# VectorE's 16 counting instructions moved from ahead of its first cast to behind its last

## The chip, the cores and the metric

The kernel runs on one core of one Trainium2 chip. The metric is the time of one execution in device microseconds; lower is better.

## The reference, cut to what matters

```python
batch, m, k, n = 16, 512, 768, 1024
# x: (batch, k, m) float32, y: (batch, k, n) float32
def reference(x, y):
    return np.einsum('bkm,bkn->bmn', x, y).astype(np.float32)
```

These are sixteen matrix products. Each loads 1.5 MB of x and 3 MB of y and stores 2 MB.

## The kernel before

SyncE issues all loads and stores. VectorE (DVE) casts each x and y tile to bfloat16. GpSimd (POOL) turns the casts' counter into one that TensorE (PE) can take from. TensorE multiplies in a loop, and ScalarE (ACT) copies the sums from PSUM to an output buffer. VectorE and ScalarE each count a semaphore `idle` up 16 times at their start. No instruction waits for it.

```python
def load(b):                                   # SyncE
    i = b % 2
    if b >= 2:
        nc.sync.wait_ge(cast, nx[b - 2])       # x buffer read by its cast
    wide_dma("x", xs[i][:], x_v[b], 4, True).then_inc(sx[i], 16)
    if b >= 2:
        nc.sync.wait_ge(cast, nx[b - 2] + parts(b - 2))
    wide_dma("y", ys[i][:], y_v[b], 2, True).then_inc(sy[i], 16)
# ... stores in batches of four, the last ones single ...

for _ in range(16):                            # VectorE
    nc.vector.sem_inc(idle, 1)
for b in range(B):
    i = b % 2
    n = 16 * (b // 2 + 1)
    if b >= 2:
        nc.vector.wait_ge(groups, 2 * (b - 1))
    nc.vector.wait_ge(sx[i], n)
    nc.vector.tensor_copy(xb[:, i], xs[i][:]).then_inc(cast, 1)
    nc.vector.wait_ge(sy[i], n)
    for h in range(parts(b)):                  # two parts for the last b, one before
        ks = slice(h * KT // parts(b), (h + 1) * KT // parts(b))
        nc.vector.tensor_copy(yb[:, i, ks], ys[i][:, ks]).then_inc(cast, 1)
# ... GpSimd and TensorE ...

nc.scalar.nop().then_inc(room, 2)              # ScalarE
for _ in range(16):
    nc.scalar.sem_inc(idle, 1)
# ... 32 copies PSUM -> ob ...
section.close()                                # a barrier of all engines
nc.sync.dma_start(o_v[B - 1, :, HB:], ob[(B - 1) % NO][:, HB:])   # the final store
```

## Time and profile before

| | before |
|---|---|
| time | 260.58 us, median of 3 (260.51 to 260.74) |
| span, first to last instruction of the profiled run | 258.8 us |
| bytes moved, mean rate | 109.07 MB, 421 GB/s |
| VectorE busy | 82.0 us, 32% |
| mean granted TensorE clock | 0.887 |

The page gives busy times by engine, then 40 slices of the span, then the transfer queues, then the chain of work that ended last. Here is the chain of the kernel before in order of time (start in us, duration in us, what).

```profile
225.47 0.27 issue
225.74 23.56 PE ps L162 x96
249.30 0.02 issue
249.32 1.86 ACT ob L178
```

The reader is to see that the last work is TensorE's matmuls of the last two batches, 48 each, and a ScalarE copy. The final store follows. VectorE's last cast lies outside of this chain.

Here is the view of SyncE's waits of before (who waited for whom: us in total, times, longest), the lines about the end:

```profile
SPq L47 <- ACTq L47: 1.9, 1, 1.9
...
SPq L47 <- PEq L47: 0.8, 1, 0.8
```

Line 47 is the barrier that closes the section, ahead of the final store. SyncE waited there for ScalarE and TensorE and not for VectorE.

### The profile page before, as it was taken

The page shows a single profiled execution, that of the slowest core. Times are in us where ns is not written, and L with a number is a line of the kernel's source. Part 1 is how long each engine was busy: PE and PEld are TensorE (multiplying, and loading weights), DVE is VectorE, ACT ScalarE, POOL GpSimd, SP SyncE. Part 2 cuts the span into 40 slices and gives each one's busy share as a digit, 9 for nine tenths or more (in the row PEclk, how much of TensorE's full clock was granted, in tenths as well). Part 3 has the DMA queues.
Part 4 walks back from the last instruction along what each step waited for, and adds up shares of the span by engine and source line. Part 5 has one row for each costly group of instructions (what it writes and reads, how often), then busy time and mean ns, then how long its engine had stood idle before and what let it go on. Part 6 is the DMA issues. An engine that isn't in the chain of part 4 may idle for free. (4 is left out here: it accounts for less than half of the span.)

```text
span 258.8 us, 2419 instructions
## 1 busy us (share of the span) xinstructions
PE 178.6 (69%) x768; PEld 88.8 (34%) x768; DVE 82.0 (32%) x33; ACT 60.9 (24%) x33; POOL 0.2 (0%) x4
## 2 busy tenths in 40 slices
PE   0019999999999007996599800999579970199950
PEld 0004555555544003553255400455235530045520
DVE  0271644527255250021643624002345272300000
ACT  1000432243220004234022002224302200413430
POOL 0000000000000000000000000000000000000000
PEclk9999999999999756999799975699979995569995
DMA  6999989898999999999999999999899999999996
GB/s 262 444 479 395 486 365 486 365 486 380 471 403 448 377 420 438 453 458 418 433 433 418 441 387 436 420 463 471 380 486 387 463 395 399 436 433 420 441 415 265
DMA packets 4658, 109.07 MB, mean 421 GB/s; under 512 B 784, under 2 KB 784, under 8 KB 784
## 3 DMA queue, kind: packets, MB, share of 16 engines
q1 hardware_dynamic: 4656, 109.06, 98.6%
q14 instruction: 2, 0.02, 0.0%
HBM read 75.50 MB, written 33.55 MB: 421 GB/s over the span
## 5 line engine op out<-in xcount | busy, mean ns | idle before, releaser
L162 PE MATMUL ps<-yb,xb 128*128 x768 | 178.6, 397 | 70.7 <-PEq L157 70.6
L162 PEld LDWEIGHTS ps<-yb,xb 128*128 x768 | 88.8, 116 | 160.0 <-issue 88.5
L178 ACT COPY ob<-ps 128x2048 f32<-128x2048 f32 x32 | 59.6, 1872 | 188.3 <-PE ps L162 126.4
L140 DVE CAST yb<-ys 128x6144 bf16<-128x6144 f32 (+1 forms) x17 | 53.8, 3171 | 80.1 <-DMA ys<-in_y_dram 80.1
L136 DVE CAST xb<-xs 128x3072 bf16<-128x3072 f32 x16 | 28.2, 1760 | 60.0 <-DMA xs<-in_x_dram 48.8
L178 ACT ACT_TABLE_LOAD x1 | 1.3, 1283 | 2.0 <-issue 2.0
L209 POOL MEMSET const-bfloat16-1.0<- 128x1 bf16 x1 | 0.1, 101 | 0.0
L209 POOL MEMSET const-uint8-127<- 128x1 uint8 x1 | 0.1, 101 | 0.0
L209 POOL MEMSET const-float32-0.0<- 128x1 f32 x1 | 0.1, 98 | 0.2 <-issue 0.2
L209 POOL MEMSET const-float32-1.0<- 128x1 f32 x1 | 0.1, 98 | 0.0
## 6 DMA issues: line engine op xcount, KB each, us to landing
ys<-in_y_dram SPq DMA_DIRECT2D x16, 3072.0 KB, 18.6
out_dram<-ob SPq DMA_DIRECT2D x15, 2048.0 KB, 27.4
xs<-in_x_dram SPq DMA_DIRECT2D x16, 1536.0 KB, 20.1
out_dram<-ob SPq DMA_DIRECT2D x2, 1024.0 KB, 7.9
```

Of the source, the lines that this page charges most:

```text
L136: nc.vector.tensor_copy(xb[:, i], xs[i][:]).then_inc(cast, 1)
L140: nc.vector.tensor_copy(yb[:, i, ks], ys[i][:, ks]).then_inc(cast, 1)
L162: mm = nc.tensor.matmul(ps[g][:, m, nt], x_w[:, bass.ds(s, 1), kt, mo], yb[:, bass.ds(s, 1), kt, nt * NF:(nt + 1) * NF], start=(kt == 0), ...
L178: cp = nc.scalar.copy(ob[b % NO][:, g * HB:(g + 1) * HB].rearrange("p m (t f) -> p m t f", f=NF), ps[g][:])
L209: nc = _bacc.Bacc("TRN2", target_bir_lowering=False, num_devices=1)
```

## The change

The intent is to let VectorE go to its first cast without counting first, and to count when its casts are done.

```diff
-    for _ in range(16):
-        nc.vector.sem_inc(idle, 1)
     for b in range(B):
         i = b % 2
         n = 16 * (b // 2 + 1)
@@
         for h in range(parts(b)):
             ks = slice(h * KT // parts(b), (h + 1) * KT // parts(b))
             nc.vector.tensor_copy(yb[:, i, ks], ys[i][:, ks]).then_inc(cast, 1)
+
+    for _ in range(16):
+        nc.vector.sem_inc(idle, 1)
```

## The prediction

> **What bounds the kernel now.** I read the page of the profile first, from its DMA rows: if the transfers fill the span, only something that moves them can matter.

> ```profile
> span 258.8 us, 2419 instructions
> PE 178.6 (69%) x768; PEld 88.8 (34%) x768; DVE 82.0 (32%) x33; ACT 60.9 (24%) x33; POOL 0.2 (0%) x4
> ...
> DMA  6999989898999999999999999999899999999996
> ...
> q1 hardware_dynamic: 4656, 109.06, 98.6%
> q14 instruction: 2, 0.02, 0.0%
> ```

> The reader is to see that the packets of the one data queue account for 98.6% of the span on 16 transfer engines, that only the first and the last of the 40 slices are clearly below full, and that VectorE (DVE) is busy for a third of the time. The kernel must move 75.50 MB in and 33.55 MB out, 109.05 MB; over the 258.8 us that is 421 GB/s. A core that is full of transfers from about 2 us to the last packet gets no shorter because an engine that waits for transfers is freed from some of its own instructions.

> Next I read the windows by stage, to see whether any stage is held by something else. Columns are PE, weight load, DVE, ACT and POOL busy with instruction counts, the granted clock, the DMA share and GB/s.

> ```profile
> 0.00:7.10 7.10, 0.00 (x0) 0.00 (x0) 0.00 (x0) 1.28 (x1) 0.20 (x4) 1.00 0.72 280
> 7.10:18.30 11.20, 0.00 (x0) 0.00 (x0) 5.34 (x3) 0.00 (x0) 0.00 (x0) 1.00 1.05 454
> ...
> 225.70:251.40 25.70, 23.54 (x96) 11.34 (x96) 0.00 (x0) 8.91 (x5) 0.00 (x0) 0.89 1.00 429
> 251.40:258.80 7.40, 0.00 (x0) 0.00 (x0) 0.00 (x0) 0.00 (x0) 0.00 (x0) 0.51 0.67 281
> ```

> The reader is to see that the DMA share is about 1.00 in the stage before the matmuls and also in the last stage with matmuls; that DVE does nothing in the first 7.1 us, which is where the 16 instructions stand now; and that it does nothing after 225.7 us, which is where they will stand. The chain that ended last names PE for its last 23.56 us, then a ScalarE copy, then the final store; no VectorE instruction is on it.

> Then the two places themselves, in three views: the lines of the counting instructions, the timeline of VectorE and SyncE at the start, and the timeline of VectorE near the end.

> ```profile
> L129 DVEq EVENT_SEMAPHORE  x16: 21/21/21, 1.0 to 2.4; - x16
> ```
> ```profile
> 0.95 0.39 SPq L75 DMA_DIRECT2D xs<-in_x_dram  x1
> ...
> 7.11 1.76 DVE L136 CAST xb<-xs 128x3072 bf16<-128x3072 f32 x1 [7.11 <-DMA xs<-in_x_dram]
> ```
> ```profile
> 218.65 3.43 DVE L140 CAST yb<-ys 128x3072 bf16<-128x3072 f32 x2 [4.92 <-DMA ys<-in_y_dram]
> ```
> ```profile
> L47 DVEq DRAIN  x1: 17/17/17, 248.5 to 248.5; - x1
> ```

> The 16 instructions start from 1.0 to 2.4 us. The first cast starts at 7.11 us and was waiting for its load, which SyncE issued at 0.95 us. The last two casts end at 218.65 + 3.43 = 222.08 us, and the next thing VectorE's queue does is a drain at 248.5 us, part of the barrier at the end of the section.

> [...] 21 ns are reported for each, but the starts are (2.4 - 1.0) / 15 = about 93 ns apart, so I cost them at the spacing and not at the reported duration. [...] I take the measured 421 over the span as what full looks like here. [...] The trace shows that queue with two packets, 0.02 MB in all, against 109.06 MB of data. No trace here says which engine asked for them.

> **The change, part by part.** It removes nothing and adds nothing; the number of instructions stays at 2419.

> Taken from the front: 16 x 93 ns = 1.5 us of VectorE's sequencer, between 1.0 and 2.4 us. After it, that sequencer stood until 7.11 us at the wait of the first cast, so 7.11 - 2.4 - 0.09 = 4.6 us of slack lay behind the counting. The cast is released by the landing of the first x tile, and SyncE, not VectorE, issues that load, at 0.95 us. VectorE will reach its wait 1.5 us earlier and stand there 1.5 us longer. Gain on the path: 0.

> Added at the back: the same 1.5 us behind the last cast. The semaphore waits that VectorE's queue does by itself (line 135) start about 0.3 us behind the end of the cast before them (29.1 against 25.39 + 3.36 = 28.75), so I put the 16 at about 222.4 to 223.9 us. The drain of the barrier comes at 248.5 us: 24.6 us of slack, 16 times what they need. The casts have incremented their own semaphore by then, so the last matmuls are not held. Cost on the path: 0.

> Who waits for the counter: nobody. The only uses of the semaphore in the program are these 16 increments and 16 on ScalarE; no wait names it. Its value can release nothing earlier or later.

> Between the two places: the casts keep their order, waits and semaphores. Load issues that wait for casts (the longest waits of SyncE: 110.9 us for the y casts, 68.4 us for the x casts) therefore come at the same times, unless the first cast moves, which it does not. Sum: 0.0 us, hence the time before, 260.58, written as 260.6.

> **The rivals.**

> *The first casts start earlier.* If the start were bound by VectorE's sequencer, up to 1.5 us, 0.6% of 260.58, could be had. Against it: the view of waits gives the load as what ended the 7.11 us of idle time, and even the 0.95 us issue is SyncE's. A gain at the start would also have to survive the full transfers of the rest. A little of it could still be real: the first four load issues take 0.39 to 0.70 us, later ones 0.47, and 16 fewer increments fly about in those microseconds. I give that at most 0.2 us, because the first issue, the quickest of them, sets when data starts. It would make about 260.4.

> *The tail becomes longer.* If VectorE came late to the closing barrier, the last store would be issued later by that. For that the counting would have to take over 24 us in place of 1.5. SyncE's waits at the barrier (view of SyncE's waits) are for ScalarE, 1.9 us, and PE, 0.8 us, and none for VectorE. If all 1.5 us stood on the path nevertheless, the time would be 262.1, still within 2%.

> *The fetch of instructions moves.* The stream behind the 16 instructions lies 16 places further ahead, so if one of the two packets is VectorE's, it will come at another time. The two hold 0.02 MB / 2 = about 8 KB each; a transfer engine moves 421 / 16 = 26 GB/s, so one packet is about 0.3 us of one of 16 engines. A transfer waits for the slowest of its 16, so up to 0.3 us either way: 260.3 to 260.9. This is the rival I hold most likely to be visible at all. If a fetch were to stop VectorE before a cast for some microseconds, it would be hidden or not by the 3.5 to 5.6 us for which VectorE waits for each y load in any case; behind the last cast it would meet the 24.6 us of slack.

> *The clock.* TensorE's granted clock is 0.887 of full on average. Nothing here changes the matmuls, so I expect the same, and the transfers hide part of it anyway.

> **How the range and the chances follow.** The three runs before lie between 260.51 and 260.74, 0.23 us apart. Around 260.6 I allow for that spread, 0.3 us for the fetch, 0.2 us at the start, and some drift between chips: 260.0 to 261.2. Two per cent are 5.2 us, more than three times all that the moved instructions take together. For "faster" or "slower" something would have to happen that no view shows; I give 0.01 and 0.02, the slower one more because an unforeseen stop of the queue can only cost. The rest, 0.97, is "same".

> **What would show each step right or wrong.** Right at the start: the first x cast again begins near 7.1 us, with the load as releaser, and the first matmul near 18.3 us. Right at the end: the 16 instructions sit between about 222.4 and 223.9 us, about 93 ns apart, the drain of VectorE again near 248.5 us, and SyncE's waits at the barrier name ScalarE and PE only. Right in between: the data queue near 98.6% and 421 GB/s. Wrong: a first cast ahead of 6.5 us, a VectorE queue that reaches the barrier last, or casts in the middle that wait for something other than loads and PE. What would make the number wrong by per cents is a different order of loads and stores in the transfer queue, set off by a small shift; the last stage with ScalarE waiting up to 21.7 us for a store is the place that I would look at first.

"That queue" is q14 of the page, with its two packets. The 421 GB/s that it takes as full are the mean of the span and its own estimate of what full is; the windows of before give 425 to 434 GB/s in the three long stages and 454 from 7.1 to 18.3 us. That a transfer waits for the slowest of its 16 is seen at the final store of before: its 16 landings came from 256.25 to 258.04 us, and SyncE's wait for it was passed at 258.06 us. The 0.2 us at the start and the drift between chips were guesses; in the rounds of e1 to e12 the medians of the kernel before were 260.71 to 260.83 us on four chips.

## The result, and the profile after

The changed kernel took 260.81 us (median of 6 runs, 260.66 to 260.92), and the kernel before took 260.69 us (median of 6, 260.51 to 260.74). The ratio is 1.0006, with a 95% interval of 0.9993 to 1.0019: the same. A ratio is worked out from the runs of both kernels in the same rounds, so it is not quite the ratio of the medians.

The page of the changed kernel answers to the lines of before like this:

```profile
span 258.9 us, 2419 instructions
PE 176.1 (68%) x768; PEld 88.3 (34%) x768; DVE 82.0 (32%) x33; ACT 60.8 (23%) x33; POOL 0.2 (0%) x4
...
q1 hardware_dynamic: 4656, 109.06, 98.6%
q14 instruction: 2, 0.02, 0.0%
```

The transfers again fill 98.6% of the span. The instruction queue again moved two packets.

The view of the counting line (now line 141), with durations in ns and the times of the first and the last start in us, and the timeline of VectorE at the first and the last casts:

```profile
L141 DVEq EVENT_SEMAPHORE  x16: 21/21/21, 218.5 to 220.3; - x16
```
```profile
7.51 1.76 DVE L134 CAST xb<-xs 128x3072 bf16<-128x3072 f32 x1 [7.51 <-DMA xs<-in_x_dram]
...
218.45 3.43 DVE L138 CAST yb<-ys 128x3072 bf16<-128x3072 f32 x2 [4.97 <-DMA ys<-in_y_dram]
```

The 16 instructions did not wait for the last casts to end. They ran beside them, from 218.5 us, while the two casts ran from 218.45 to 221.88 us. The first cast again waited for its load, but that load landed 0.4 us later than in the profile of before (7.51 against 7.11). Whether the change did that had to be tested. TensorE's granted clock was 0.885 to 0.898 in the six runs of the changed kernel, against 0.883 to 0.903 in the nine of the kernel before in the rounds of e1 to e4: no difference that could be told.

In SyncE's waits of the changed kernel only ScalarE is left at the barrier. The first line is the wait for the final store, which e8 will need, and the second view shows when that store was issued:

```profile
SPq L221 <- DMA out_dram<-ob: 7.1, 1, 7.1
...
SPq L47 <- ACTq L47: 1.8, 1, 1.8
```
```profile
250.68 0.33 SPq L195 DMA_DIRECT2D out_dram<-ob  x1
```

The raw records of the instruction queue show that one of its packets has moved. They are times in us from the span's start; each packet is 8192 bytes and took 0.31 to 0.33 us:

```
before   215.36   248.25
after    223.79   247.45
```

### The profile page after: what moved, and what is told of

The parts are those of the page before. It is cut to its first block, busy times and chain, and to the rows that moved or that the text cites. A ratio compares the mean times of both kernels' runs of the same rounds, so it can differ in the third digit from the quotient of the medians.

```text
span 258.9 us, 2419 instructions
## 1 busy us (share of the span) xinstructions
PE 176.1 (68%) x768; PEld 88.3 (34%) x768; DVE 82.0 (32%) x33; ACT 60.8 (23%) x33; POOL 0.2 (0%) x4
## 3 DMA queue, kind: packets, MB, share of 16 engines
q1 hardware_dynamic: 4656, 109.06, 98.6%
HBM read 75.50 MB, written 33.55 MB: 421 GB/s over the span
## 5 line engine op out<-in xcount | busy, mean ns | idle before, releaser
L163 PE MATMUL ps<-yb,xb 128*128 x768 | 176.1, 392 | 72.4 <-PEq L158 72.4
```

The lines of the kernel that those rows point to most:

```text
L163: mm = nc.tensor.matmul(ps[g][:, m, nt], x_w[:, bass.ds(s, 1), kt, mo], yb[:, bass.ds(s, 1), kt, nt * NF:(nt + 1) * NF], start=(kt == 0), ...
```

## The experiments

The theory was that the 16 instructions are hidden at both places. The rivals were that they cost or save something at the start, that they cost something at the end, that the moved instruction packet matters, and later that their number matters. Each table row is one kernel of its own. "Before" is the kernel before on the same chip in the same rounds. "Outside" is the time less the span of the same run, so what an execution takes outside of the program's own first and last instruction. "VectorE" is the number of its instructions in the trace. The spans on record are rounded to 0.1 us, so one value of "outside" is good to 0.05 us. The profiled runs have the span to a nanosecond: there it is 1.77 to 1.78 us in every kernel with 65, 71, 295 or 455 VectorE instructions and 2.11 to 2.17 us in every kernel with 55, 183 or 311.

| run | VectorE | time, us | before, us | ratio (95%) | mean span, this / before | outside, us |
|---|---|---|---|---|---|---|
| e1, before once more | 71 | 260.63 | 260.78 | 0.9998 (0.9984 to 1.0012) | 258.94 / 258.99 | 1.73 to 1.82 |
| e2, after once more | 71 | 260.81 | 260.78 | 0.9997 (0.9983 to 1.0010) | 258.98 / 258.99 | 1.74 to 1.81 |
| e3, none on VectorE | 55 | 261.13 | 260.78 | 1.0012 (0.9998 to 1.0025) | 258.92 / 258.99 | 2.13 to 2.23 |
| e4, none on both | 55 | 261.21 | 260.78 | 1.0013 (0.9999 to 1.0026) | 258.98 / 258.99 | 2.14 to 2.23 |
| e5, 16 ahead of each x cast | 311 | 261.38 | 260.71 | 1.0025 (1.0008 to 1.0042) | 259.23 / 258.91 | 2.11 to 2.15 |
| e6, 128 in front | 183 | 261.15 | 260.71 | 1.0013 (0.9996 to 1.0030) | 258.98 / 258.91 | 2.09 to 2.17 |
| e7, 240 behind | 295 | 261.62 | 260.71 | 1.0036 (1.0019 to 1.0053) | 259.85 / 258.91 | 1.73 to 1.81 |
| e8, 400 behind | 455 | 263.89 | 260.71 | 1.0124 (1.0107 to 1.0141) | 262.15 / 258.91 | 1.73 to 1.81 |
| e9, 240 empty instructions (fell out) | 55 | 261.37 | 260.83 | 1.0026 (1.0011 to 1.0041) | 259.23 / 258.94 | 2.12 to 2.26 |
| e10, 240 on GpSimd | 71 | 261.71 | 260.83 | 1.0033 (1.0018 to 1.0049) | 259.85 / 258.94 | 1.73 to 1.83 |
| e11, none on VectorE again | 55 | 261.12 | 260.83 | 1.0016 (1.0002 to 1.0030) | 258.98 / 258.94 | 2.13 to 2.26 |
| e12, 10 in front | 65 | 261.02 | 260.79 | 1.0010 (0.9996 to 1.0024) | 259.28 / 259.03 | 1.76 to 1.82 |

The outside part of the kernel before was 1.73 to 1.83 us in all its runs of all rounds.

### e1 and e2: both kernels once more

No edit. What was expected of the kernel before:

> The kernel before once more, as a measure of what two identical kernels differ by. Every theory: ratio 1.000, within 0.1%. Open: the first x cast began at 7.11 us in the profile of before and at 7.51 us in that of after. If the landing of the first load varies from run to run, it may begin anywhere from 7.0 to 7.6 us here; if the moved instructions set it, it begins at 7.1 us again.

And of the changed one:

> The changed kernel once more. Theory (the 16 instructions are hidden at both places): ratio 0.999 to 1.001 against before. Rival (they cost or save something small at one place): a ratio off 1 by more than the identical kernel shows, 1.0005 or more with an interval that leaves out 1. The first x cast begins at 7.5 us if the change sets it, anywhere from 7.0 to 7.6 us if it is chance. One instruction packet near 223.8 us, one near 247 to 248 us.

Both gave a ratio within 0.03% of 1, with intervals of 0.13 to 0.14% either way. The 1.0006 of the first comparison can't be told from that. The first cast, in the timelines of VectorE of the two:

```profile
7.41 1.76 DVE L136 CAST xb<-xs 128x3072 bf16<-128x3072 f32 x1 [7.41 <-DMA xs<-in_x_dram]
```
```profile
7.67 1.76 DVE L134 CAST xb<-xs 128x3072 bf16<-128x3072 f32 x1 [7.67 <-DMA xs<-in_x_dram]
```

The unchanged kernel began at 7.41 us this time, so 7.11 is not a property of the program. Together with the first two profiles that is 7.11 and 7.41 us with the 16 in front, 7.51 and 7.67 us without, which looks like an effect of the change. The later traces settle it: with 10 or 16 in front the first cast also began at 7.29 (e12), 7.62 (e10) and 7.72 us (e5), and with none in front at 7.37 to 7.58 us (e3, e4, e7, e8, e9, e11). The two sets overlap, so the landing varies by chance.

### e3, e4 and e11: the 16 taken out

```diff
-    for _ in range(16):
-        nc.vector.sem_inc(idle, 1)
```

e4 takes ScalarE's 16 out as well.

> VectorE's 16 increments taken out altogether, ScalarE's kept. Theory: 260.5 to 260.9 us, ratio within 0.1% of 1. Rival of the front place (1.5 us lie on the path): 259.1 us. Rival of the fetch: if one of the two instruction packets belongs to VectorE's stream (71 instructions in the trace, 55 here), it is gone and one packet is left; if it does not, both remain at about the times of before.

> The 16 increments of ScalarE taken out as well. Theory: 260.5 to 260.9 us again. ScalarE's first work is at 26 us, its 16 increments take 1.1 us of the first 2 us. If the second instruction packet is ScalarE's (70 instructions in the trace, 54 here), no instruction packet is left within the span. Rival (fetches hold a transfer up): 0.3 to 0.6 us faster than before.

> The kernel without VectorE's 16 increments, a second time: it showed 261.13 us against 260.78 us of before, with an interval of 0.9998 to 1.0025 that holds 1. If that was chance of a load or of the chip's condition, the ratio is now 0.9995 to 1.0005; if leaving the 16 out costs something, it is 1.0010 to 1.0015 again and e4's 1.0013 was the same effect.

Here I was surprised. Taking the instructions away made nothing faster. The second time the interval left out 1, on the slow side: 1.0016. The span explains nothing of it (258.92 against 258.99 us in e3, 258.98 against 258.94 in e11). The whole 0.4 us is in the part outside: 2.13 to 2.26 us against 1.73 to 1.83, two sets that do not touch. So leaving out work that nobody waits for cost 0.4 us, and it did so outside of the span. My expectation for e3 and e4, 260.5 to 260.9 us, was missed by 0.2 to 0.3 us. In e4 the part outside is the same as in e3, so taking ScalarE's 16 out added nothing to it.

The instruction queue shows whose packets they are. The pages of e3 and e4:

```profile
span 259.0 us, 2403 instructions
```
```profile
span 259.2 us, 2387 instructions
```

In e3's records the packet near 215 or 224 us is gone and the one near 247 us is left; in e4's there is none. The first packet belongs to VectorE's stream, the second to ScalarE's.

### e5 and e6: VectorE held up in the middle and at the start

```diff
+    # e5: none in front, but in the loop, ahead of each x cast
+        for _ in range(16):
+            nc.vector.sem_inc(idle, 1)
```
```diff
-    for _ in range(16):
+    for _ in range(128):     # e6, in front
         nc.vector.sem_inc(idle, 1)
```

> 16 increments ahead of each of the 16 x casts, 256 in all in place of 16, each set about 16 x 93 ns = 1.5 us. Theory (VectorE's time is hidden behind full transfers all along): within 1 us of before, so 260 to 262 us, though the x casts begin up to 1.5 us later behind a y cast. Rival (VectorE's queue is on the path between the ends): each set adds its 1.5 us, 15 x 1.5 = 22 us, about 283 us. Between: the casts near the end, where the last x and y gate the last matmuls, could add 1.5 us once, 262 us.

> 128 increments ahead of the first cast: 128 x 93 ns = 11.9 us, from 1.0 to about 12.9 us, 5.4 to 5.8 us past the landing of the first x tile. Theory (a late first cast is hidden as well, since 9.4 MB, some 22 us of transfers, are in the queue by then): the first cast begins near 12.9 us, and the total grows by at most 1 us. Rival (the start is on the path once the slack of 4.6 us is used up): 260.6 + 5.5 = 266 us.

In e6 the first cast came late, and the profile says that its load was not the reason. Timeline of VectorE in e6:

```profile
13.25 1.76 DVE L136 CAST xb<-xs 128x3072 bf16<-128x3072 f32 x1 [13.25 <-issue]
15.12 3.36 DVE L140 CAST yb<-ys 128x6144 bf16<-128x6144 f32 x1
18.81 1.76 DVE L136 CAST xb<-xs 128x3072 bf16<-128x3072 f32 x1 [0.33 <-DMA xs<-in_x_dram]
```

The idle time of 13.25 us now ends by "issue", which means that VectorE waited for nothing but its own queue. The third cast is on time again. The mean span grew by 0.06 us for a first cast that was 5.8 us later than the 7.41 of e1. In e5, where 256 instructions of 93 ns (23.8 us in all) were spread over the whole run, it grew by 0.31 us, which is little more than the 0.25 us between two kernels with the same instructions (e9 and e11 below). The rest of both totals is again outside the span, 0.35 us. So at the start and in the middle VectorE has microseconds to spare, as the theory has it.

### e7 and e8: many behind the last cast

```diff
-    for _ in range(16):
+    for _ in range(240):     # e7; 400 in e8, behind the last cast
         nc.vector.sem_inc(idle, 1)
```

> 240 increments behind the last cast: 22.3 us from 218.5 us, so to about 241 us, ahead of the barrier at 248.5 us. Theory: 260.5 to 261 us, no change. If they begin only when the last cast has ended (222.4 us), they end at 244.7 us: no change either. Rival (instructions at the back hold up the end in any case[...]): over 261.5 us.

> 400 increments behind the last cast: 37.1 us from 218.5 us, to 255.6 us (or 259.5 us if they begin when the last cast has ended). Theory: VectorE now reaches the barrier last; the final store, issued at 250.7 to 251.4 us before, is issued near 256 us, and the total is 264 to 266 us, with VectorE named in SyncE's waits at the barrier. Rival (the barrier does not hang on VectorE): 260.7 us as before.

With 400 the barrier was reached late. SyncE's waits of e8:

```profile
SPq L47 <- DVEq L47: 7.3, 1, 7.3
...
SPq L221 <- DMA out_dram<-ob: 3.6, 1, 3.6
```
```profile
257.38 0.33 SPq L195 DMA_DIRECT2D out_dram<-ob  x1
```

VectorE is now named at the barrier. The final store was issued at 257.38 us, 6.7 us later than the 250.68 us of the changed kernel, and the time grew by only 3.2 us, a little under what I expected. The last line of the first view says why. In the changed kernel SyncE waited 7.1 us for the final store, because stores ahead of it were still in the queue (they landed until 255.72 us); here they had all landed by 257.08 us, and it waited 3.6 us. About 3.5 us of the delay were bought back in this way. So the rival about the tail is real, but for the barrier to be late it needs some 28 us of instructions (an estimate: from 220.3 us, where the 16 ended, to the drain at 248.6 us) and not 1.5.

With 240 the instructions ended at 241.5 us, well ahead of the barrier, and SyncE did not wait for VectorE there. Still the mean span was 0.94 us longer. So the 261.62 us missed my 260.5 to 261 and lay where I had put the rival (over 261.5). The landings of the final store show where: 14 of its 16 transfer engines were done by 257.21 us, one at 257.96, the last at 259.06. In the kernel before the fifteenth was done at 257.44 and the last at 258.04. One engine is last by 0.1 to 1.1 us in the other traces too, but there it is done by 258.44 us at the latest (e8, where the final store was issued late, and e10 below aside). The time was lost while the 240 ran: from the landing of the store at 223.5 us to that of the third store after it passed 15.55 us, against 14.71 in the kernel before, 14.91 in the changed one, and 14.52 to 14.97 in all traces but those of e8 (15.56) and e10 (15.63). I had not foreseen such a cost ahead of the barrier.

### e9 and e10: what the 240 have in common

```diff
-    for _ in range(16):
-        nc.vector.sem_inc(idle, 1)
+    for _ in range(240):     # e9, behind the last cast
+        nc.vector.nop()
```
```diff
             nc.gpsimd.wait_ge(cast, nx[b] + h + 1).then_inc(ready, 2 // parts(b))
+    for _ in range(240):     # e10, VectorE as before
+        nc.gpsimd.sem_inc(idle, 1)
```

> As the 240 behind the last cast, but each increment replaced by an instruction of VectorE's sequencer that does nothing and touches no semaphore. The 240 increments cost 0.9 us (ratio 1.0036), seen as one of the 16 transfer engines falling behind by about 0.2 us per store between 218 and 241 us. Theory A (each sequencer instruction that is run, or the record of it, loads that engine): 261.4 to 261.8 us again. Theory B (the increment of a semaphore does it): 260.5 to 261.0 us.

> 16 increments of VectorE in front as before, and 240 increments on GpSimd behind its last counting of a cast, from 222.1 us on. Theory A and B alike, if it is the number of instructions or of increments: 261.3 to 261.8 us. Theory C (it is VectorE's queue that matters[...]): 260.5 to 261.0 us.

e9 failed as an experiment. Its trace holds 55 VectorE instructions, as many as without any counting: the empty instructions did not get into the program. It became a third run without the 16, and agrees with the other two in the part outside, 2.12 to 2.26 us. Its mean span was 0.28 us longer than that of before, and 0.25 us longer than that of e11, whose trace holds the same instructions; nothing here explains that, and a difference of this size in the mean span proves nothing by itself. e9 does not tell theory A from theory B.

e10 gave 261.71 us. Its span grew by 0.91 us, as in e7, and again one transfer engine was late: the fifteenth was done at 257.39 us, the last at 259.16. So it does not take VectorE's place or queue; 240 increments on GpSimd do the same. The instruction packets are not the whole reason: the store between 228.7 and 234.0 us saw no instruction packet in either run and took 5.19 and 5.17 us from landing to landing, against 4.84 to 5.00 us for the same store in the profiles with 16 or none behind the casts. Whether the increments, or the recording of each instruction in the trace, load that engine stays open; every run here was recorded. For the 16 it would be 16/240 of 0.9 us, 0.06 us, an estimate from e7 and below what these rounds can tell.

### e12: where the number of instructions falls

What separates the kernels with 1.8 us outside from those with 2.2? Starts of VectorE's counting instructions lie 93 ns apart, but in the traces of five kernels there is a stop in the row, with 0.44 to 0.50 us from one start to the next: between VectorE's instructions 63 and 64, in the order of its queue, in the changed kernel, e5, e6, e7 and e8, in e7 and e8 again between 191 and 192, and in e8 every 128 after that. I call these places edges; they lie 128 instructions apart. With 71, 295 or 455 instructions the last edge lies inside the span. With 55, 183 or 311 the next edge is eight instructions behind the last one of the span. With 295 the next one is 24 behind, and the part outside is not longer; so on this account, an estimate from these counts, VectorE runs at least 8 and fewer than 24 instructions behind the span.

The packets bear the edges out. GpSimd's 240 in e10 have two such stops as well, of 0.42 and 0.39 us, 128 instructions apart, in a row with 78 ns from start to start (222.24 to 241.61 us in all). In every trace but that of e12, told of below, the number of 8192-byte packets within the span is that of the edges passed by VectorE, ScalarE and GpSimd: two in the kernel before, the changed one and e6, three in e5 and e7, four in e10, five in e8, one in e3, e9 and e11, none in e4. Where a stop can be seen in a row of increments, the packet starts 0.9 to 5.0 us after it has ended. So the stop is not a wait for that packet; what the sequencer does in it stays open.

If that stop, 0.35 to 0.41 us beyond the usual spacing, is the cause, a kernel with 65 must show it inside the span, between VectorE's wait in the closing barrier and the drain behind it.

```diff
-    for _ in range(16):
+    for _ in range(10):      # in front
         nc.vector.sem_inc(idle, 1)
```

The raw records of VectorE's last instructions (start in us, duration in ns, what):

```
before
258.343  21  EVENT_SEMAPHORE
258.453  10  DRAIN
258.787  21  EVENT_SEMAPHORE
e12
258.325  21  EVENT_SEMAPHORE
258.835 134  DRAIN
259.134  21  EVENT_SEMAPHORE
```

The gap is 0.51 us in place of 0.11, at the instruction that was named in advance. The same in the views of the closing line, before and then e12 (times of first and last start at the end):

```profile
L220 DVEq DRAIN  x2: 10/10/10, 248.6 to 258.5; - x2
...
L220 DVEq EVENT_SEMAPHORE  x2: 21/21/21, 258.3 to 258.8; - x2
```
```profile
L220 DVEq DRAIN  x2: 10/72/134, 248.6 to 258.8; - x2
...
L220 DVEq EVENT_SEMAPHORE  x2: 21/21/21, 258.3 to 259.1; - x2
```

The wait at 258.3 us is passed at the same time in both, and the last one is 0.35 us later. The packets agree: e12 has ScalarE's packet alone within the span, at 247.96 us, and one more that starts 0.33 us behind the span's end, the only one there in any of the traces. The part outside went back to 1.76 to 1.82 us and the mean span grew by 0.25 us, where I expected 0.3. The time, 261.02 us, is near what was expected; its ratio (1.0010) and the 0.25 us of span prove nothing alone, the position of the stop does. No instruction is recorded outside of the span, and no packet behind it in e3, e4, e5, e6, e9 or e11, so for these the same cause is inferred: from the 0.35 to 0.4 us, from the counts, and from the stop appearing in the span when the count is moved.

No run suggests a version that beats both kernels, so none was tried.

## Why the prediction was right

The prediction of 260.6 us, range 260.0 to 261.2, held: 260.81 us. Its sum of 0.0 us held too: no difference could be told from that of a kernel against itself.

**The front.** Right. The 1.5 us were hidden behind the first load; e6 shows that even 12 us there cost 0.06 us of span. The mark that I gave for it, a first cast near 7.1 us, was a poor one: the landing varies from 7.1 to 7.7 us from run to run, with the 16 in front or without them.

**The rival of quicker issues at the start.** It found nothing: the changed kernel's first four load issues took 0.39, 0.42, 0.54 and 0.64 us, against 0.39, 0.42, 0.53 and 0.70 before.

**The back.** The cost of 0 was right, the place was wrong. I put the instructions at 222.4 to 223.9 us (and, reading the stages, behind 225.7 us, which does not fit with that), because the waits of line 135 start 0.3 us behind a cast. That was a misreading. In the trace of before each of the 14 waits starts 27 or 28 ns after the landing of the x tile that it names, and two of them start 19.8 us behind the cast: they waited for loads and not for the cast to end. The 16 ran at 218.5 to 220.3 us, beside the casts. VectorE's queue went on to them while a cast ran: the first increment starts at 218.469 us, 15 ns behind the start of a cast of 1.76 us. The slack to the barrier is 28 us rather than 24.6, and e8 shows what happens when it is used up.

**The moved fetch.** Right that it would be VectorE's packet and that it would be visible: it went from 215.4 to 223.8 us. The up to 0.3 us that I allowed for it do not show in the totals, where an identical kernel differs as much.

**Small misreadings.** The prediction has ScalarE wait up to 21.7 us for a store in the last stage; the wait there is 20.02 us. It ends the chain with the final store, which the view does not list. Neither enters the sum.

**What the prediction did not see.** It did say that a stop of VectorE by a fetch would be hidden in its waits, and in both kernels the edge did lie in a wait or beside a cast. But it treated the instructions as free to have or to lack. They are not: without them 0.4 us are added outside of the span (2.12 to 2.26 us against 1.73 to 1.83), most likely because the stop at an edge is then not hidden (0.51 us in place of 0.11 in e12), while the 16 place it inside the span, where a wait or a cast covers it. The change keeps their number and so keeps this; that part was luck, since the prediction asked nothing about it. Had the change been to delete them, the same reasoning would have given 260.6 us, and the runs gave 261.1.

## What to carry to other kernels

When a profile shows an engine waiting for a transfer on both sides of some instructions, test a move from one wait to the other by multiplying them until the slack is used up: here moving 16 changed nothing (1.0006, 0.9993 to 1.0019), and 400 cost 3.2 us. Before deleting instructions that seem to do nothing, look at the time outside of the span as well as in it: here their number most likely put a stop of about 0.4 us in VectorE's queue where it was hidden. When a difference of 0.1% matters, run the same kernel against itself first.
